# Moving the normalisation and turning of eight token tiles from the second layer's start into the first layer's attention

## The chip, the cores and the metric

The kernel is one program on one core of a Trainium2 chip. The metric is its time on the device in microseconds (us), the median of several runs. Its engines are TensorE (PE in the profile; PEld is its loading of weights), VectorE (DVE), ScalarE (ACT), GpSimd (POOL) and SyncE (SP, which here issues nearly all DMAs). Each engine executes its own instructions in order and waits on semaphores for the others.

## The reference

A two-layer backbone over 1024 latent tokens and 256 context tokens of width 1024, float32. The first layer's mixer is a windowed grouped-query attention, the second's a latent attention; each layer is `x += gate * mixer(norm(x) * (1 + scale) + shift)`.

```python
for i in range(DEPTH):                       # DEPTH = 2
    hx = rms_norm(x, norm_g[i]) * (1.0 + scale_x[:, None]) + shift_x[:, None]
    hc = rms_norm(ctx, norm_g[i]) * (1.0 + scale_c) + shift_c
    if kind == 0:
        yx, yc = window_gqa(hx, hc, a_w_in[j], a_sink[j], a_w_out[j], cos_a, sin_a, need_ctx)
    elif kind == 1:
        yx, yc = latent_attention(hx, hc, b_w_in[j], b_q_norm[j], ..., need_ctx)
    x = x + gate_x[:, None] * yx
    if need_ctx:
        ctx = ctx + gate_c * yc
return rms_norm(x, final_g)

def latent_attention(...):
    def project(h):
        cq, ckv, kr, g = jnp.split(h @ w_in, [...], axis=-1)
        q = (rms_norm(cq, q_norm) @ w_uq)...
        kv = (rms_norm(ckv, kv_norm) @ w_ukv)...
    ...
```

What matters here is the seam: the second layer needs h = norm(x1) * A + B of the first layer's output x1, transposed, so that the model width lies on partitions, for its input products `h @ w_in`.

## The kernel before

All on-chip memory is managed by hand: `arena_f` (float32) and `arena_r` (the operands of products) are cut into frames with `f_at(offset in KB, ...)` and `r_at`, and a `Ring` hands out a list of frames in turn. A ring of three frames therefore lets the fourth user start only when the first is done with its frame. `PB` is the accumulator memory (PSUM) of eight banks; `Banks` hands banks out in turn. Float32 products are made of three products of high and low parts (`mm3`, L126 to L128); `split` (L121, L122) makes such parts: a cast on ACT gives the high part, a subtract on DVE or POOL the low part.

The tokens are ten tiles of 128, two of context (0 and 1) and eight latent ones. The attention of the first layer runs over 40 units (`units`), a tile times one of four key groups, in the tile order `ORDER = (2, 0, 3, 1, 4, 5, 6, 7, 8, 9)`. A unit computes scores (L586), a masked maximum on DVE (L597), the exponential on ACT (L600), the transposes of P on PE (`T`, L617; split by L121 on ACT and L122 on DVE), the product with V (`PV`, L627) and its finish (`fin`, `fin2`). The output projection of a tile (`outproj`, L126 to L128 with 512 columns) is a generator, advanced a few products at a time between the steps of the next tile's units (`filler`). Its end multiplies by the gate (L674), adds to x (L675) and stores the tile of x1 (L676). The last tile's projection runs behind the last unit (`last_outproj`), and its second half accumulates in bank 0.

Behind it the second layer starts. `fetch1` loads weights in pieces through the ring `stg` (L264) and splits them; `build_x` handles a pair of tiles p: `norm_x` loads a tile of x1 (L212), sums its squares on ACT (L214), takes the reciprocal root (L215 on DVE, L216 on POOL) and scales the tile on DVE (L217); `turn_x` transposes it in eight steps on PE (L224) and copies two PSUM banks out on ACT (L225). `build_h` makes h of the pair: eight affine steps on DVE (L238), four casts on ACT (L241) and four subtracts (L243). Then `kv_tile` (24 products of 288 columns a tile, a norm at L958 to L997, transposes at L1010) runs over the ten tiles and `g_tile` (48 products of 256 columns) after each second latent one; between them, ahead of tile ti, tile ti + 3 is turned, and its pair's h is built. The written order is not the executed one to the letter: a scheduler merges the instructions of an engine, so places are shown below as they stand in the engines' own queues.

Of the kernel before, what the change touches and what calls it, by code (L numbers as in the profile page):

```python
# [60 lines left out]
def kernel(ctx: ExitStack, tc: tile.TileContext, t, out, dbg=None):  # L61
# [14 lines left out]
    x1_d = dpool.tile([TOK, D], F32, name="x1_d")  # L76
    qn_d = dpool.tile([8, 128, 2, SEQ], F32, name="qn_d")
# [132 lines left out]
    def norm_x(src, xr, junk):  # L210
        x = xr.next()
        load(out=x, in_=src)  # L212
        st = sm_ring()
# [4 lines left out]
        return x  # L218

    def turn_x(x, xt, j):  # L220
        for q in range(2):
            ps = shp(pst(), 4, 128)
            for c in range(4):
                nc.tensor.transpose(ps[:, c, :], x[:, (4 * q + c) * 128 : (4 * q + c + 1) * 128], ident)  # L224
            nc.scalar.copy(xt[:, 4 * q : 4 * q + 4, j * 128 : j * 128 + 128], ps)  # L225

    def build_x(p, src, xr, xtr, junk):

        xt = shp(xtr.next(), 8, 256)
        for j in range(2):  # L230
            turn_x(norm_x(src(2 * p + j), xr, junk), xt, j)
        return xt

    def build_h(p, xt, hT, A, B, fast=False, ks=range(8)):

        w = 1 if p == 0 else 0
        for k in ks:
            nc.vector.tensor_scalar(xt[:, k, :], xt[:, k, :], A[:, k, w : w + 1], B[:, k, w : w + 1], ALU.mult, ALU.add)  # L238
            if k % 2:
                hi = hT[:, 0, k - 1 : k + 1, :]  # L240
                nc.scalar.copy(hi, xt[:, k - 1 : k + 1, :])  # L241
                eng = nc.vector if fast or k % 4 == 1 else nc.gpsimd
                eng.tensor_sub(hT[:, 1, k - 1 : k + 1, :], xt[:, k - 1 : k + 1, :], hi.bitcast(F32))  # L243
# [434 lines left out]
    units = [UnitA(ti, g) for ti in ORDER for g in range(4)]  # L678

# [193 lines left out]
    for ui, u in enumerate(units):  # L873
# [11 lines left out]
        for ci in range(u.m):  # L885
# [90 lines left out]
    fetch1(1)  # L976
# [123 lines left out]
    nx = norm_x(src1(4), xr, junk)  # L1100
    for ti in range(NT):
        n = ti + 3
        if 4 <= n < NT:
            if n % 2 == 0:
                xt = shp(xtr.next(), 8, 256)
            turn_x(nx, xt, n % 2)
            if n + 1 < NT:
# [568 lines left out]
```

## Time and profile before

| | |
|---|---|
| median of 3 runs (lowest, highest) | 1596.19 us (1595.39, 1599.35) |
| profiled execution | 1596.15 us |
| its span | 1594.4 us |
| mean granted TensorE clock | 0.997 |
| PE, DVE, ACT, POOL busy, share of the span | 98%, 57%, 49%, 47% |
| last product with V of the attention (L627) starts | 715.68 us |
| output projection of the last tile (PE) | 716.28 to 730.47 us |
| first kv product of the second layer | 730.47 us |

Times in rows are microseconds from the start of the span. A wait row gives engine, buffer and line, the releasing engine and line, then the total in us, the number of times, and the longest. In a row of groups the mean duration in ns stands behind the busy time. A timeline row has start, duration, engine, line, operation, and in brackets idle time of the engine before it with what ended it.

### The profile page before, as it was taken

The page shows a single profiled execution, that of the slowest core. Times are in us where ns is not written, and L with a number is a line of the kernel's source. Part 1 is how long each engine was busy: PE and PEld are TensorE (multiplying, and loading weights), DVE is VectorE, ACT ScalarE, POOL GpSimd, SP SyncE. Part 2 cuts the span into 40 slices and gives each one's busy share as a digit, 9 for nine tenths or more (in the row PEclk, how much of TensorE's full clock was granted, in tenths as well). Part 3 has the DMA queues.
Part 4 walks back from the last instruction along what each step waited for, and adds up shares of the span by engine and source line. Part 5 has one row for each costly group of instructions (what it writes and reads, how often), then busy time and mean ns, then how long its engine had stood idle before and what let it go on. Part 6 is the DMA issues. An engine that isn't in the chain of part 4 may idle for free.

```text
span 1594.4 us, 26916 instructions
## 1 busy us (share of the span) xinstructions
PE 1555.2 (98%) x9938; PEld 1222.6 (77%) x9938; DVE 905.9 (57%) x1629; ACT 777.0 (49%) x1478; POOL 742.1 (47%) x805
## 2 busy tenths in 40 slices
PE   7899999999999999998999999999999999999998
PEld 4787777887878888887998899766766766766687
DVE  3515551618777777768525302667677677667454
ACT  3522232348777777767523332455545555555322
POOL 1231112115664444454113350388688688689510
PEclk9999999999999999999999999999999999999999
DMA  7446776354333333327113753313232233244251
GB/s 253 166 138 196 233 210 190 97 153 120 109 110 94 97 93 94 93 79 244 35 34 106 262 184 94 103 30 101 69 96 80 76 88 96 67 130 118 67 167 66
DMA packets 147203, 192.82 MB, mean 121 GB/s; under 512 B 13936, under 2 KB 84080, under 8 KB 147072
## 3 DMA queue, kind: packets, MB, share of 16 engines
q1 hardware_dynamic: 145456, 188.94, 39.5%
q10 hardware_dynamic: 1616, 2.17, 0.5%
q8 instruction: 78, 1.28, 0.4%
q14 instruction: 53, 0.43, 0.1%
HBM read 144.90 MB, written 46.15 MB: 120 GB/s over the span
## 4 chain that ended last, share of the span: by engine, by line
PE 86%; issue 2%; DVE 2%; POOL 2%; ACT 2%; DMA 1%; SPq 0%; POOLq 0%; DVEq 0%; ACTq 0%
PE PB L126 15%; PE PB L127 14%; PE PB L128 14%; PE PB L1303 11%; PE PB L1325 8%; PE PB L586 5%; PE PB L627 4%; PE PB L1266 4%; PE PB L617 4%; PE PB L183 1%; PE PB L1274 1%; PE PB L1354 1%; PE PB L646 1%; ACT arena_r L121 1%; DVE arena_r L122 1%
## 5 line engine op out<-in xcount | busy, mean ns | idle before, releaser
L126 PE MATMUL PB<-arena_r 128*128 128x512 f32 (+3 forms) x1496 | 509.9, 342 | 4.9 <-POOL arena_r L653 2.0
L127 PE MATMUL PB<-arena_r 128*128 128x512 f32 (+3 forms) x1496 | 502.4, 336 | 4.2 <-DVE arena_r L390 2.1
L128 PE MATMUL PB<-arena_r 128*128 128x512 f32 (+3 forms) x1496 | 500.3, 335 | 0.3 <-DVE arena_r L122 0.3
L1317 POOL TENSOR_TENSOR arena_f<-arena_f 128x512 f32<-128x512 f32 x252 | 328.3, 1303 | 82.1 <-ACT arena_f L1309 65.3
L126 PEld LDWEIGHTS PB<-arena_r 128*128 128x128 f32 x1496 | 283.7, 190 | 52.7 <-issue 12.5
L127 PEld LDWEIGHTS PB<-arena_r 128*128 128x128 f32 x1496 | 284.5, 190 | 32.0 <-DVE arena_r L390 3.5
L128 PEld LDWEIGHTS PB<-arena_r 128*128 128x128 f32 x1496 | 284.5, 190 | 28.3 <-DVE arena_r L122 0.5
L122 POOL TENSOR_TENSOR arena_r<-arena_f,arena_r 128x512 fp32r<-128x512 f32 x88 | 115.2, 1325 | 299.7 <-ACT arena_r L121 255.5
L1309 ACT ACTIVATE arena_f<-PB 128x1024 f32<-128x1024 f32 x160 | 164.1, 1027 | 108.9 <-PE PB L1303 65.9
L1268 DVE TENSOR_REDUCE arena_f<-PB 128x1 f32<-128x1024 f32 x128 | 156.1, 1219 | 86.7 <-PE PB L1266 86.6
L1303 PE MATMUL PB<-arena_r 64*128 64x512 f32 (+1 forms) x1600 | 202.3, 392 | 0.3 <-ACT arena_f L1309 0.3
L1303 PEld LDWEIGHTS PB<-arena_r 64*128 64x128 f32 (+1 forms) x1600 | 146.1, 185 | 31.5 <-ACT arena_f L1309 1.8
L122 DVE TENSOR_TENSOR arena_r<-PB,arena_r 128x512 fp32r<-128x512 f32 (+1 forms) x186 | 124.2, 674 | 61.9 <-ACT arena_r L121 61.0
L1325 PE MATMUL PB<-arena_f 128*64 128x512 f32 x640 | 144.4, 597 | 0.0
L600 ACT ACTIVATE arena_f<-arena_f,small 128x640 f32<-128x640 f32 (+2 forms) x160 | 119.5, 747 | 35.4 <-DVE small L597 32.7
L597 DVE CUSTOM_DVE_ANT_0 arena_f<-PB,arena_f,small 128x640 f32<-128x640 f32 (+2 forms) x176 | 125.2, 722 | 20.1 <-PE PB L586 12.6
L121 ACT CAST arena_r<-PB 128x512 fp32r<-128x512 f32 (+1 forms) x186 | 105.3, 573 | 47.4 <-PE PB L617 45.2
L121 ACT CAST arena_r<-arena_f 128x512 fp32r<-128x512 f32 (+3 forms) x141 | 83.8, 603 | 86.7 <-PE PB L128 12.5
L627 PE MATMUL PB<-arena_r 128*128 128x512 f32 x336 | 115.8, 429 | 0.5 <-DVE arena_f L639 0.5
L586 PE MATMUL PB<-arena_r 128*128 128x256 f32 (+1 forms) x576 | 111.0, 308 | 1.6 <-DVE small L597 1.3
L1325 PEld LDWEIGHTS PB<-arena_f 128*64 128x64 f32 x640 | 43.1, 136 | 83.2 <-issue 79.9
L617 PE MATMUL PB<-ident,arena_f 128*128 128x128 f32 x672 | 104.2, 274 | 1.3 <-DVE arena_r L122 0.8
(177 smaller groups left out, 1842.9 us busy)
## 6 DMA issues: line engine op xcount, KB each, us to landing
arena_f<-ada_w SPq DMA_DIRECT2D x47, 512.0 KB, 5.4
arena_r<-q_d SPq DMA_DIRECT2D x80, 256.0 KB, 3.9
arena_r<-qn_d SPq DMA_DIRECT2D x64, 256.0 KB, 3.9
arena_r<-qr_d SPq DMA_DIRECT2D x192, 64.0 KB, 3.3
arena_f<-a_w_in SPq DMA_DIRECT2D x40, 256.0 KB, 3.6
arena_f<-x SPq DMA_DIRECT2D x16, 512.0 KB, 6.6
g_d<-arena_f SPq DMA_DIRECT2D x32, 256.0 KB, 2.1
q_d<-arena_f SPq DMA_DIRECT2D x64, 128.0 KB, 2.4
```

Source lines behind the costliest of these rows:

```text
L121: nc.scalar.copy(hi, src)
L122: (lo_eng or nc.vector).tensor_sub(lo, src, hi.bitcast(F32))
L126: nc.tensor.matmul(o, ah, bh, start=first, stop=False)
L127: nc.tensor.matmul(o, al, bh, start=False, stop=False)
L128: nc.tensor.matmul(o, ah, bl, start=False, stop=last)
L586: nc.tensor.matmul(S[:, at : at + n], qT[:, s, hq, :], kT[:, g, k : k + n], start=s == 0, stop=s == 1)
L617: nc.tensor.transpose(pt[:, h, :], self.Ps[h][:, ci * 128 : ci * 128 + 128], ident)
L627: nc.tensor.matmul(self.pv, V[:, self.chunks[ci], self.g, :], PT[:, s], start=ci == 0 and s == 0, stop=ci == self.m - 1 and s == 1,)
L1303: nc.tensor.matmul(S[:, t], k[r, c : c + 128], q[r], start=j == 0, stop=j == 4)
L1309: nc.scalar.activation(E, self.S, AF.Exp)
L1317: eng.tensor_add(self.acc, self.acc, E[:, t])
L1325: nc.tensor.matmul(self.pv[p : p + 64], Vq[:, cs[t], self.h % 4, :], E[:, t], start=i == 0, stop=i == 4)
```

## The change

Tiles 0 to 7 are normalised and turned inside the attention, by a generator `pre_turns` that is advanced behind the tiles at positions 5 to 9 of `ORDER` (two steps a unit, one at position 8). Its steps per tile are: load x1 into `xpre` and, a step later, the scaling; then four transposes, a PSUM copy into one of two staging buffers `tpre` and a store to DRAM (`xT_d`), twice. The turned pairs are loaded back in two halves of 512 KB each (`load_xt`): pair 0 at unit 38, pairs 1 and 2 at the start of the second layer, pair 3 ahead of the kv tiles. Only tiles 8 and 9 are turned between the kv tiles, as before. `build_h` works on halves of a pair (four affine steps, two casts, two subtracts); pairs 2, 3 and 4 are built in halves behind kv tiles 0, 1, 2, 3, 5 and 6 (`part`). The weights of block 1 (for cq) are fetched behind tile 3, not ahead of the loop. To make room, the weight ring `stg` (three frames still), the gate ring `gr` and other frames move.

```diff
@@ helpers
     def norm_x(src, xr, junk):
         x = xr.next()
         load(out=x, in_=src)
+        scale_x(x, junk)
+        return x
+
+    def scale_x(x, junk):
         st = sm_ring()
         ...
-            nc.scalar.copy(xt[:, 4 * q : 4 * q + 4, j * 128 : j * 128 + 128], ps)
+            nc.scalar.copy(xt[q][:, :, j * 128 : j * 128 + 128], ps)
-    def build_x(p, src, xr, xtr, junk):
-        ...
     def build_h(p, xt, hT, A, B, fast=False, ks=range(8)):
         ...
-            nc.vector.tensor_scalar(xt[:, k, :], xt[:, k, :], A[:, k, w : w + 1], ...)
+            x = xt[k // 4][:, k % 4, :]
+            nc.vector.tensor_scalar(x, x, A[:, k, w : w + 1], B[:, k, w : w + 1], ALU.mult, ALU.add)
@@ attention
-    or1, rtr = (Ring(F, [o, o - 5], 256) for o in (43, 45))
+    or1, rtr = Ring(F, [43, 44], 256), Ring(F, [45, 41], 256)
-    gr = Ring(F, [2.5, 34, 46], 256)
+    gr = Ring(F, [34, 35, 46], 256)
+    xpre, tpre = f_at(48, 1024), [f_at(o, 4, 128) for o in (36, 38)]
+
+    def pre_turn(ti):
+        load(out=xpre, in_=x1_d[ti * 128 : ti * 128 + 128, :])
+        yield
+        scale_x(xpre, f_at(36, 512).bitcast(BF16))
+        yield
+        for q in range(2):
+            ps = shp(pst3(), 4, 128)
+            for c in range(4):
+                k = 4 * q + c
+                nc.tensor.transpose(ps[:, c, :], xpre[:, k * 128 : k * 128 + 128], ident)
+            nc.scalar.copy(tpre[q], ps)
+            ts = slice(ti % 2 * 128, ti % 2 * 128 + 128)
+            load(out=xT_d[ti // 2, :, 4 * q : 4 * q + 4, ts], in_=tpre[q])
+            yield
+    ...
+    xt_at = [[f_at(o, 4, 256) for o in os] for os in ((48, 36), (14, 18), (22, 26), (14, 18), (22, 26))]
+
+    def load_xt(p):
+        for q in range(2):
+            load(out=xt_at[p][q], in_=xT_d[p, :, 4 * q : 4 * q + 4, :])
@@ end of each unit
+        for _ in range({5: 2, 6: 2, 7: 2, 8: 1, 9: 2}.get(ui // 4, 0)):
+            next(pre, None)
+        if ui == 38:
+            load_xt(0)
         u.fin(og)
@@ second layer
-    junk = f_at(34.5, 512).bitcast(BF16)
-    stg = Ring(F, [30, 32.25, 49.5], 576)
-    xr = Ring(F, [22, 26, 45], 1024)
-    xtr = Ring(F, [14, 37], 2048)
+    junk = f_at(40, 512).bitcast(BF16)
+    stg = Ring(F, [30, 32, 44], 512)
+    xr = Ring(F, [48, 36], 1024)
     fetch1(0, nc.vector)
-    xts = {0: build_x(0, src1, xr, xtr, junk)}
-    build_h(0, xts.pop(0), hT1[0], ada1.A, ada1.B, fast=True)
-    xts[1] = build_x(1, src1, xr, xtr, junk)
-    build_h(1, xts.pop(1), hT1[1], ada1.A, ada1.B, fast=True)
+    load_xt(1)
+    build_h(0, xt_at[0], hT1[0], ada1.A, ada1.B, fast=True)
+    load_xt(2)
+    build_h(1, xt_at[1], hT1[1], ada1.A, ada1.B, fast=True)
     ...
     fetch1(6)
-    fetch1(1)
-    nx = norm_x(src1(4), xr, junk)
+    load_xt(3)
+    nx = {8: norm_x(src1(8), xr, junk)}
     for ti in range(NT):
-        n = ti + 3
-        if 4 <= n < NT:
-            ...
+        if ti in (4, 5):
+            turn_x(nx[ti + 4], xt_at[4], ti % 2)
         kv_tile(ti)
         flush(2)
+        part = {0: (2, 0), 1: (2, 4), 2: (3, 0), 3: (3, 4), 5: (4, 0), 6: (4, 4)}
+        if ti in part:
+            p, k = part[ti]
+            build_h(p, xt_at[p], hT1[p], ada1.A, ada1.B, True, range(k, k + 4))
+        if ti == 1:
+            nx[9] = norm_x(src1(9), xr, junk)
+        if ti == 3:
+            fetch1(1)
         if ti > 1 and ti % 2:
             g_tile(6, ti // 2)
-    qst = Ring(F, [16, 20, 24, 37, 41, 45], 1024)
+    qst = Ring(F, [16, 20, 24, 36, 48, 8], 1024)
```

Most line numbers shift: the three products are L127 to L129 in the changed kernel, the subtract of a split L123, the affine step L236, the subtract of h L242, the gate multiply L673, the x1 store L675, the weight loads L263; the pre-turning transposes are L689, their stores L692, the load of x1 for them L681, the reload L703.

The first place is PE's queue where the output projection of the last tile ends and the kv products of the second layer start (512 columns are the projection, 288 the kv tiles, L224 the turning). Before:

```order
L126 MATMUL PB<-arena_r 128x288
L127 MATMUL PB<-arena_r 128x288
L128 MATMUL PB<-arena_r 128x288
L126 MATMUL PB<-arena_r 128x288
L224 MATMUL PB<-ident,arena_f 128x128 x8
L127 MATMUL PB<-arena_r 128x288
```

Now:

```order
L128 MATMUL PB<-arena_r 128x512
L129 MATMUL PB<-arena_r 128x512
L127 MATMUL PB<-arena_r 128x288
L128 MATMUL PB<-arena_r 128x288
L129 MATMUL PB<-arena_r 128x288
```

The turning transposes, which stood between and among the kv products, are gone from here, so one kind of product follows the other directly.

They stand in the attention instead; this is PE in one of the last units (L616 transposes of P, L626 the product with V, L585 scores, L645 the finish):

```order
L626 MATMUL PB<-arena_r 128x512 x2
L585 MATMUL PB<-arena_r 128x256 x4
L689 MATMUL PB<-ident,arena_f 128x128 x4
L585 MATMUL PB<-arena_r 128x256 x4
L616 MATMUL PB<-ident,arena_f 128x128 x3
L645 MATMUL PB<-ident,arena_f 128x128 x2
L616 MATMUL PB<-ident,arena_f 128x128
L585 MATMUL PB<-arena_r 128x256 x2
L616 MATMUL PB<-ident,arena_f 128x128
```

The four L689 are half a tile's turning, between score products.

The second place is DVE's queue around the gate multiply of the last output projection (L674, then the add L675; L673 and L674 now). Subtracts of 288 columns belong to kv weights, L238 (L236 now) and L243 (L242 now) to h, L217 and L215 to the norm of a tile. Before:

```order
L243 TENSOR_TENSOR arena_r<-arena_f,arena_r 128x512
L238 TENSOR_SCALAR arena_f<-arena_f,small 128x256 x2
L217 TENSOR_SCALAR arena_f<-arena_f,small 128x1024
L215 TENSOR_SCALAR small<-small 128x1
L674 TENSOR_TENSOR arena_f<-PB,arena_f 128x512
L243 TENSOR_TENSOR arena_r<-arena_f,arena_r 128x512
L217 TENSOR_SCALAR arena_f<-arena_f,small 128x1024
L675 TENSOR_TENSOR arena_f<-arena_f 128x512
L215 TENSOR_SCALAR small<-small 128x1
L674 TENSOR_TENSOR arena_f<-PB,arena_f 128x512
L217 TENSOR_SCALAR arena_f<-arena_f,small 128x1024
```

Now:

```order
L242 TENSOR_TENSOR arena_r<-arena_f,arena_r 128x512
L236 TENSOR_SCALAR arena_f<-arena_f,small 128x256
L242 TENSOR_TENSOR arena_r<-arena_f,arena_r 128x512
L123 TENSOR_TENSOR arena_r<-arena_f,arena_r 128x288 x2
L673 TENSOR_TENSOR arena_f<-PB,arena_f 128x512
L236 TENSOR_SCALAR arena_f<-arena_f,small 128x256
L674 TENSOR_TENSOR arena_f<-arena_f 128x512
L236 TENSOR_SCALAR arena_f<-arena_f,small 128x256
L673 TENSOR_TENSOR arena_f<-PB,arena_f 128x512
L123 TENSOR_TENSOR arena_r<-arena_f,arena_r 128x288
L674 TENSOR_TENSOR arena_f<-arena_f 128x512
L1003 TENSOR_SCALAR arena_f<-arena_f 128x512
```

The norm's steps left; two subtracts of weights and h of the second pair now stand directly ahead of the first multiply, and affine steps stand between the two multiplies.

The third place is SP's queue around the first weights of the second layer (x_d<- is a store of a tile of x1, <-x_d the load of a tile of x1, xT_d the turned tiles, b_w_in weights, g_d and q_d the attention's operands, <-x the projection's residual). Before:

```order
L676 DMA x_d<-arena_f 128x1024
L658 DMA arena_f<-x 128x1024
L570 DMA arena_f<-g_d 128x2x128 x2
L212 DMA arena_f<-x_d 128x1024
L264 DMA arena_f<-b_w_in 128x288 x2
L212 DMA arena_f<-x_d 128x1024
L676 DMA x_d<-arena_f 128x1024
L264 DMA arena_f<-b_w_in 128x288 x3
L212 DMA arena_f<-x_d 128x1024
L658 DMA arena_f<-x 128x1024
L264 DMA arena_f<-b_w_in 128x288 x2
L212 DMA arena_f<-x_d 128x1024
```

Now:

```order
L703 DMA arena_f<-xT_d 128x1024
L692 DMA xT_d<-arena_f 128x4x128 x2
L703 DMA arena_f<-xT_d 128x1024 x4
L263 DMA arena_f<-b_w_in 128x288 x2
L703 DMA arena_f<-xT_d 128x1024
L675 DMA x_d<-arena_f 128x1024
L263 DMA arena_f<-b_w_in 128x288 x3
L657 DMA arena_f<-x 128x1024
L263 DMA arena_f<-b_w_in 128x288 x2
L703 DMA arena_f<-xT_d 128x1024
L263 DMA arena_f<-b_w_in 128x288
L703 DMA arena_f<-xT_d 128x1024
```

The loads of x1 between the weights have become reloads of turned halves; five of those of the first pairs, and the last two stores of turned halves, stand ahead of the first weights.

More of the change, by code (lines that the diff above doesn't have):

```diff
@@ L76 @@
     x1_d = dpool.tile([TOK, D], F32, name="x1_d")
+    xT_d = dpool.tile([4, 128, 8, 256], F32, name="xT_d")
     qn_d = dpool.tile([8, 128, 2, SEQ], F32, name="qn_d")
@@ L678, with pre_turns @@
     units = [UnitA(ti, g) for ti in ORDER for g in range(4)]
+    xpre, tpre = f_at(48, 1024), [f_at(o, 4, 128) for o in (36, 38)]
[13 more added lines that the diff above has]
+            yield
+    def pre_turns():
+        for ti in range(8):
+            yield from pre_turn(ti)
+    xt_at = [[f_at(o, 4, 256) for o in os] for os in ((48, 36), (14, 18), (22, 26), (14, 18), (22, 26))]
+    def load_xt(p):
+        for q in range(2):
+            load(out=xt_at[p][q], in_=xT_d[p, :, 4 * q : 4 * q + 4, :])
+    pre = pre_turns()
     def wo_load():
```

18 lines of the change are left out of this document (3 added, 15 removed).

## The prediction

> **What bounds the kernel now.** I read the head of the page first, then its chain, then busy time by stretches around the hand-over from the first layer to the second, and last what TensorE (PE) waited for there.
>
> ```profile
> span 1594.4 us, 26916 instructions
> PE 1555.2 (98%) x9938; PEld 1222.6 (77%) x9938; DVE 905.9 (57%) x1629; ACT 777.0 (49%) x1478; POOL 742.1 (47%) x805
> PE 86%; issue 2%; DVE 2%; POOL 2%; ACT 2%; DMA 1%; SPq 0%; POOLq 0%; DVEq 0%; ACTq 0%
> ```
>
> The profiled execution took 1596.15 us, 1.75 us more than its span and practically the median of the three runs (1596.19), so a difference worked out in the trace can be put on the median as it stands. PE is busy 98% of the span and carries 86% of the chain: only PE work removed, or PE idle time closed or opened, moves the end. Columns below: stretch, its length, busy time of PE, PEld, DVE, ACT and POOL, the granted TensorE clock, DMA share, GB/s.
>
> ```profile
> 520.00:640.00 120.00, 119.80 (x717) 103.06 (x716) 92.19 (x185) 87.56 (x203) 58.85 (x102) 1.00 0.33 93
> 716.00:731.00 15.00, 14.40 (x72) 11.26 (x71) 12.26 (x32) 12.28 (x27) 3.01 (x4) 1.00 0.89 295
> 731.00:804.00 73.00, 65.83 (x510) 64.43 (x509) 49.77 (x127) 41.01 (x89) 25.12 (x35) 0.98 0.35 107
> 804.00:900.00 96.00, 95.69 (x636) 87.09 (x635) 35.30 (x69) 26.01 (x54) 24.76 (x24) 1.00 0.37 113
> ```
>
> The first attention (here 520 to 640) leaves PE 0.2 us idle in 120; behind 804 it is full again. Between lie 88 us with about 7.8 us of idle PE and a clock under 1. That is the stretch in which all ten tiles are normalised and turned now. The waits in it, each once:
>
> ```profile
> PE PB L1010 <- ACT arena_f L225: 3.3, 1, 3.3
> PE PB L224 <- DVE small L959: 1.2, 1, 1.2
> PE PB L126 <- ACT arena_r L241: 1.1, 1, 1.1
> PE PB L224 <- DVE arena_f L217: 0.9, 1, 0.9
> PE PB L127 <- DVE arena_r L243: 0.6, 1, 0.6
> PE PB L224 <- DVE small L215: 0.5, 1, 0.5
> ```
>
> All six belong to the chain norm, transposes, affine, cast, subtract of a tile (L215 to L243), or stand behind it. The longest also costs clock:
>
> ```profile
> 755.00:758.20 3.20, 0.00 (x0) 0.00 (x0) 3.20 (x9) 2.62 (x6) 0.00 (x0) 0.92 0.58 157
> 758.20:760.00 1.80, 1.77 (x9) 1.78 (x10) 1.80 (x7) 1.77 (x6) 0.10 (x1) 0.50 0.00 0
> 760.00:762.00 2.00, 2.00 (x14) 2.00 (x14) 1.66 (x6) 1.07 (x3) 1.53 (x3) 0.72 0.00 0
> ```
>
> **What goes.** The six waits are 3.3 + 1.2 + 1.1 + 0.9 + 0.6 + 0.5 = 7.6 us. The half clock loses 1.80 x 0.50 + 2.00 x 0.28 = 1.46, say 1.4. Together 9.0 us, if nothing takes their place.
>
> **What moves.** 64 of the 80 PE transposes go into the attention, where PE is full, so they cost there what they save later.
>
> ```profile
> 716.28 0.91 PE L126 MATMUL PB<-arena_r 128*128 128x512 f32 x2
> 725.69 0.39 PE L126 MATMUL PB<-arena_r 128*128 128x512 f32 x1
> 730.47 0.29 PE L126 MATMUL PB<-arena_r 128*128 128x288 f32 x1
> 730.60 0.29 PE L127 MATMUL PB<-arena_r 128*128 128x288 f32 x1
> 731.61 1.09 PE L224 MATMUL PB<-ident,arena_f 128*128 128x128 f32 x8
> 732.45 0.38 PE L127 MATMUL PB<-arena_r 128*128 128x288 f32 x1
> ```
>
> Eight take 732.45 - 731.61 = 0.84 us, so 64 are 6.7 us on either side: zero in the sum. A 128x288 product is issued every 0.13 us (730.60 - 730.47), a 128x512 one every 0.228 (21 of them from 725.69 to 730.47).
>
> **What the attention pays.** Per tile it also gets a Square, two PSUM copies, a scaling on DVE and a reciprocal root on POOL; 1.06 + 0.19 + 2 x 0.59 = 2.4 us of ACT and 0.75 of DVE, by these groups (mean ns in the middle):
>
> ```profile
> L225 ACT COPY arena_f<-PB 128x512 f32<-128x512 f32 x20 | 11.2, 585 | 2.4 <-PE PB L224 2.4
> L214 ACT ACTIVATE arena_f<-arena_f 128x1024 bf16<-128x1024 f32 x10 | 10.6, 1059 | 0.7 <-DMA arena_f<-x_d 0.5
> L214 ACT ACTIVATION_READ_ACCUMULATOR arena_f<-arena_f 128x1 f32 x10 | 1.9, 190 | 0.0
> L217 DVE TENSOR_SCALAR arena_f<-arena_f,small 128x1024 f32<-128x1024 f32 x10 | 7.5, 753 | 4.5 <-POOL small L216 4.4
> ```
>
> ACT is 73% busy there (87.56 of 120) and would be 77 to 79%. What counts is how far it runs ahead of PE:
>
> ```profile
> ACT arena_r L121 <- PE PB L617: 27.8, 47, 0.8
> DVE arena_r L122 <- ACT arena_r L121: 34.0, 46, 1.7
> PE PB L617 <- ACT arena_f L600: 0.2, 1, 0.2
> ```
>
> These are of 520 to 700. Before its cast of a transposed P tile, ACT stands 27.8 / 47 = 0.59 us waiting for PE, so a Square of 1.25 us can make a cast 0.66 late, and a copy of 0.59 can just be swallowed. Eight Squares give at most 5.3 us. Against that, output-projection products stand between the transposes of P and their use, and the 0.2 us row shows no lateness with the attention's own copies in place. I take 0.15 us a tile, 1.2 us, nearest to that row; ends 0 and 5.3. The pre-transposes share two PSUM banks with the transposes of P (a part of the same term: a bank is held by a 0.59 copy as it is by the 0.59 cast). DMA: 8 loads of 512 KB move forward; 16 stores of 256 KB and 8 loads of 512 KB are new, on the one SP queue, past the q and gate loads. The share there is 0.33; nothing of PE waits for a load in these rows, so 0. POOL, busy 58.85 us of 120, gets one 128x1 operation a tile: 0.
>
> **At the end of the attention.** DVE does affine steps in 0.35 us each (725.23), in 0.70 where POOL works on tiles beside it (751.16):
>
> ```profile
> 715.95 0.69 DVE L674 TENSOR_TENSOR arena_f<-PB,arena_f 128x512 f32<-128x512 f32 x1 [1.07 <-PE PB L128]
> 725.23 1.38 DVE L238 TENSOR_SCALAR arena_f<-arena_f,small 128x256 f32<-128x256 f32 x4 [0.54 <-ACT arena_f L225]
> 751.16 5.60 DVE L238 TENSOR_SCALAR arena_f<-arena_f,small 128x256 f32<-128x256 f32 x8
> ```
>
> Four of them, for tile pair 1, stand now ahead of the last subtract of P: 1.4 us, less part of the 1.07 that DVE idles there. I take 0.5; ends 0 and 2.8 (four at 0.70).
>
> **The new first wait.** (Times on the clock of the trace before, the moved 6.7 us left out.) Without transposes the output projection of tile 9 takes 48 x 0.228 = 10.9 us from 716.3, so PE is at the kv products at 727.2 instead of 730.47, and 13 of them later (1.7 us) at 728.9. Then it needs PSUM bank 0, which the multiply of the output projection empties on DVE (L674; L673 in the changed kernel). That one now stands behind the subtracts of the last two kv weight pieces:
>
> ```profile
> 723.84 0.80 SPq L264 DMA_DIRECT2D arena_f<-b_w_in  x2
> 727.59 0.43 ACT L121 CAST arena_r<-arena_f 128x288 fp32r<-128x288 f32 x1 [0.20 <-DMA arena_f<-b_w_in]
> 728.58 0.69 DVE L243 TENSOR_TENSOR arena_r<-arena_f,arena_r 128x512 fp32r<-128x512 f32 x1
> 729.18 0.45 DVE L122 TENSOR_TENSOR arena_r<-arena_f,arena_r 128x288 fp32r<-128x288 f32 x1
> 731.64 0.69 DVE L674 TENSOR_TENSOR arena_f<-PB,arena_f 128x512 f32<-128x512 f32 x1
> 744.42 0.42 DVE L973 TENSOR_SCALAR arena_f<-arena_f 128x512 f32<-128x512 f32 x1
> ```
>
> The weights are issued at 723.84, cast from 727.59 (3.75 us later), subtracted until 729.6. A ring of three buffers holds them back, and it has three in the new kernel too, so these times stay; without the 0.6 us between the two subtracts, they end at 729.1. Behind come a multiply, two affine steps, an add, and the second multiply; at the 0.6 us at which such operations follow each other (728.58 to 729.18) 0.6 + 2 x 0.35 + 0.6 + 0.6 = 2.5, which makes 731.6 or 731.7. PE stands from 728.9 to 731.7: 2.8 us. Ends: 0 (before, PE lost nothing to weights, its transposes lying over that time) and 4.3, if the landing takes 1.5 us longer because the reloads of the turned tiles share the DMA engines (their share is 0.89 in this stretch).
>
> **The new second wait.** In place of the 3.3 us, the first transpose of a normalised kv tile waits for its DVE chain, behind the scaling of b_q_norm (L973), a load that lands late, and behind h of pair 2. ACT issues that load at 732.81 now and some 3.2 us earlier, 729.6, without the last Squares and copies ahead of it (two tiles at 2.4 us, less ACT's waits); the nearest row for its landing is the last:
>
> ```profile
> 732.81 0.38 ACTq L972 DMA_DIRECT2D arena_f<-b_q_norm  x1
> arena_f<-b_kv_norm ACTq DMA_DIRECT2D x1, 128.0 KB, 5.3
> ```
>
> 729.6 + 5.3 = 734.9; with 0.42 for the scaling, three subtracts (2.0), five affine steps at 0.35 to 0.70 (2.6) and the tile's own norm (1.4, an estimate from the 1.2 us that PE waits on such a norm now) it is about 741.3. PE has 72 - 13 = 59 products left from 731.7, to 739.6. Idle 1.8 us; ends 0 and 3.5.
>
> The sum: -9.0 + 1.2 + 0.5 + 2.8 + 1.8 = -2.7, so 1596.2 - 2.7 = 1593.5 us. The loop behind, with h in halves (four affine steps and two subtracts on DVE between two kv tiles, not eight and four), I cost at nothing: a half is 4 x 0.35 to 0.70 + 2 x 0.69 = 2.8 to 4.2 us of DVE, and the cover is a kv tile of 24 x 0.13 = 3.2 us and, behind each odd one, a gate tile. If that cover failed, the 1.0 us over, four times, would be added. The second layer's weights for cq, fetched later (behind tile 3), are first read behind the whole loop: 0.
>
> **The clock, weighed.** Row: 3.3 us of idleness gave 0.50; the other waits, up to 1.2 us, cost no clock, since the 1.46 us lost behind it are all of the 0.02 that 731 to 804 lacks. The new 2.8 us lies between; with the clock kept the sum is 1593.5, with it lost 1594.9. [...]
>
> **Rivals.**
> (1) The cover holds: weights and b_q_norm come early enough, and the two new waits are 0.5 us each. -9.0 + 1.2 + 0.5 + 1.0 = -6.3: 1590. For it: in the stretch ACT has 24 operations fewer, DVE 16. Against: the 3.75 us from issue to cast has a row. Chance 0.30.
> (2) The new waits are as long as the old. With bank 0 at +4.3 (over 3.3, so the clock falls: 1.4) and 3.0 at the second: -9.0 + 1.2 + 0.5 + 4.3 + 1.4 + 3.0 = +1.4: 1597.6. For it: DMA share 0.89. Chance 0.20.
> (3) Slower: the Squares land on casts that PE needs. It decides when a cast becomes late by over 1.0 us a tile: 8 x 1.25 (no slack at all) = 10 in place of 1.2, so -2.7 + 8.8 = +6.1: 1602.3. For it: ACT executes in order, at 73%. Against: 0.59 us of slack per cast, and PE's 0.2. Chance 0.12.
> The likeliest stays the sum, 1593.5 (chance 0.38, between 1590.8 and 1596).
>
> **From chances to numbers.** A measurement tells 0.3%, 4.8 us, from no change, so faster means below 1591.4 and slower above 1601.0. Faster: rival 1, and the low end of the sum, 0.30 + 0.08 = 0.38. Slower: rival 3 and the high end of rival 2, 0.12 + 0.03 = 0.15. Same: the rest, 0.47. The range goes from 1587.5 (every new term near its lower end: -9.0 makes 1587.2) to 1601.0 (rival 2 with three tenths of what rival 3 adds to the attention, 1597.6 + 2.6 = 1600.2, and up to the bound of slower); it leaves out the 0.15 above and 0.05 below.
>
> **What would show it.** In the trace after: PE's waits at L1010 on the copy L225 and the 0.50 clock are gone (first step); the attention 6.7 us longer, with PE waits under 2 us (second); kv products from about 727 + 6.7, with one wait near the 13th (third) and one at the first transpose of a kv tile (fourth). Wrong if PE waits on casts (L122) in the attention row by row, or if no wait stands where the weights arrive.

## The result: 1.3% slower, and the profile after

The changed kernel takes 1617.26 us (1615.89 to 1620.10), the kernel before, with one run more than the prediction had, 1597.73 us; the ratio is 1.0126, 95% interval 1.0105 to 1.0147. The forecast was 1593.5, with a range up to 1601.0. The head of the page after:

```profile
span 1616.0 us, 26933 instructions
PE 1562.3 (97%) x9938; PEld 1225.6 (76%) x9938; DVE 890.8 (55%) x1629; ACT 776.5 (48%) x1478; POOL 747.2 (46%) x805
PE 77%; issue 5%; DVE 4%; POOL 4%; ACT 3%; DMA 3%; POOLq 0%; SPq 0%; DVEq 0%; ACTq 0%
```

PE's share of the chain fell from 86% to 77%: other engines and transfers hold PE up now. To see where, I cut each span at two marks that all kernels have, the issue of the x1 store of tile 1 and that of tile 8. Between them lies the attention with the turning (called S below), behind them the rest. Before, then after, in the columns of the prediction's stretches:

```profile
524.13:718.04 193.91, 193.27 (x1154) 165.28 (x1153) 146.30 (x297) 139.31 (x327) 97.75 (x166) 1.00 0.31 91
718.04:1594.40 876.36, 858.34 (x5921) 654.64 (x5919) 493.46 (x740) 391.65 (x609) 475.05 (x405) 1.00 0.35 105
```

```profile
524.42:748.10 223.68, 206.15 (x1221) 172.81 (x1220) 159.35 (x329) 159.23 (x366) 104.03 (x174) 0.99 0.43 126
748.10:1616.00 867.90, 850.75 (x5854) 648.63 (x5852) 465.50 (x709) 370.99 (x569) 473.69 (x397) 0.99 0.35 103
```

The rest gained 8.5 us (876.36 - 867.90). S lost 29.8: PE is busy 12.9 us longer and idle 17.5 us instead of 0.6. What PE waited for in S after:

```profile
PE PB L585 <- DVE small L596: 7.2, 3, 2.9
PE PB L616 <- DVE arena_r L123: 4.7, 4, 1.7
PE PB L626 <- DVE arena_f L638: 4.4, 4, 2.9
```

These three rows are 16.3 of the 17.5 us, all on VectorE, at scores, transposes of P and products with V. The 2.9 us in the last row are one wait at the end of the attention, which is taken up below. What VectorE and ScalarE themselves waited for in the turning (L219 Square, L220 mean, L221 root on POOL, L222 scaling):

```profile
DVE small L220 <- ACT arena_f L219: 18.4, 7, 3.7
ACT arena_f L219 <- DMA arena_f<-x_d: 6.4, 4, 2.5
ACT arena_f L219 <- DMA xT_d<-arena_f: 5.7, 3, 2.1
DVE arena_f L222 <- POOL small L221: 4.9, 8, 0.7
```

VectorE stood 18.4 + 4.9 = 23.3 us. In its queue mean and scaling follow each other directly in seven of the eight tiles, with the attention's work behind them:

```order
L123 TENSOR_TENSOR arena_r<-PB,arena_r 128x512
L220 TENSOR_SCALAR small<-small 128x1
L222 TENSOR_SCALAR arena_f<-arena_f,small 128x1024
L123 TENSOR_TENSOR arena_r<-PB,arena_r 128x512
L596 ISA arena_f,small<-PB,arena_f,small 128x640
```

One such place in the timelines of SP, ACT, DVE and PE:

```profile
572.81 0.41 SPq L681 DMA_DIRECT2D arena_f<-x_d  x1
578.26 1.06 ACT L219 ACTIVATE arena_f<-arena_f 128x1024 bf16<-128x1024 f32 x1 [1.59 <-DMA arena_f<-x_d]
579.44 0.15 DVE L220 TENSOR_SCALAR small<-small 128x1 f32<-128x1 f32 x1 [2.05 <-ACT arena_f L219]
580.27 0.75 DVE L222 TENSOR_SCALAR arena_f<-arena_f,small 128x1024 f32<-128x1024 f32 x1 [0.68 <-POOL small L221]
582.48 1.03 PE L585 MATMUL PB<-arena_r 128*128 128x256 f32 x4 [2.06 <-DVE small L596]
```

The load of the tile is issued at 572.81, after the tile before has left its frame, and the Square starts on it 5.45 us later. ScalarE has reached the Square and waits; VectorE waits for the Square from 577.4 on, then for the root; the subtract and the maximum that PE needs run only behind the scaling, and PE stands 2.06 us.

### The profile page after: what moved, and what is told of

Read it like the earlier page. It is cut to its first block, busy times and chain, and to the rows that moved or that the text cites. A ratio compares the mean times of both kernels' runs of the same rounds, so it can differ in the third digit from the quotient of the medians.

```text
span 1616.0 us, 26933 instructions
## 1 busy us (share of the span) xinstructions
PE 1562.3 (97%) x9938; PEld 1225.6 (76%) x9938; DVE 890.8 (55%) x1629; ACT 776.5 (48%) x1478; POOL 747.2 (46%) x805
## 4 chain that ended last, share of the span: by engine, by line
PE 77%; issue 5%; DVE 4%; POOL 4%; ACT 3%; DMA 3%; POOLq 0%; SPq 0%; DVEq 0%; ACTq 0%
PE PB L127 14%; PE PB L128 13%; PE PB L129 13%; PE PB L1334 11%; PE PB L1356 8%; PE PB L1297 4%; PE PB L585 3%; PE PB L626 3%; PE PB L616 2%; DVE arena_r L123 1%; DMA xT_d<-arena_f 1%; PE PB L184 1%; DVE arena_f L596 1%; ACT arena_r L122 1%; PE PB L1305 1%
## 5 line engine op out<-in xcount | busy, mean ns | idle before, releaser
L127 PE MATMUL PB<-arena_r 128*128 128x512 f32 (+3 forms) x1496 | 510.0, 342 | 5.0 <-POOL arena_r L652 2.0
L129 PE MATMUL PB<-arena_r 128*128 128x512 f32 (+3 forms) x1496 | 501.0, 335 | 0.2 <-DVE arena_r L123 0.2
L1348 POOL TENSOR_TENSOR arena_f<-arena_f 128x512 f32<-128x512 f32 x252 | 324.6, 1288 | 79.4 <-ACT arena_f L1340 62.6
L127 PEld LDWEIGHTS PB<-arena_r 128*128 128x128 f32 x1496 | 284.5, 191 | 52.6 <-issue 12.5
L129 PEld LDWEIGHTS PB<-arena_r 128*128 128x128 f32 x1496 | 285.4, 191 | 28.3 <-DVE arena_r L123 0.5
L123 POOL TENSOR_TENSOR arena_r<-arena_f,arena_r 128x512 fp32r<-128x512 f32 x88 | 115.4, 1325 | 309.6 <-ACT arena_r L122 255.5
L123 DVE TENSOR_TENSOR arena_r<-PB,arena_r 128x512 fp32r<-128x512 f32 (+1 forms) x186 | 123.6, 673 | 53.0 <-ACT arena_r L122 52.0
L626 PE MATMUL PB<-arena_r 128*128 128x512 f32 x336 | 118.8, 435 | 5.6 <-DVE arena_f L638 4.8
L585 PE MATMUL PB<-arena_r 128*128 128x256 f32 (+1 forms) x576 | 113.3, 311 | 8.7 <-DVE small L596 8.4
L122 ACT CAST arena_r<-PB 128x512 fp32r<-128x512 f32 (+1 forms) x186 | 105.1, 572 | 30.8 <-PE PB L616 29.8
L616 PE MATMUL PB<-ident,arena_f 128*128 128x128 f32 x672 | 106.4, 275 | 5.8 <-DVE arena_r L123 5.5
```

What stands on the lines that cost most here:

```text
L122: nc.scalar.copy(hi, src)
L123: (lo_eng or nc.vector).tensor_sub(lo, src, hi.bitcast(F32))
L127: nc.tensor.matmul(o, ah, bh, start=first, stop=False)
L129: nc.tensor.matmul(o, ah, bl, start=False, stop=last)
L585: nc.tensor.matmul(S[:, at : at + n], qT[:, s, hq, :], kT[:, g, k : k + n], start=s == 0, stop=s == 1)
L626: nc.tensor.matmul(self.pv, V[:, self.chunks[ci], self.g, :], PT[:, s], start=ci == 0 and s == 0, stop=ci == self.m - 1 and s == 1,)
```

## The experiments

Lengths of S, PE's idle time in S (length less busy, from the same view), the part of S in which the trace's record of the granted clock has 0.50, and the rest, in us, each from one profiled execution; the time is the median of the runs. The part ahead of S, which no edit is about, differs between these executions by up to 4.3 us (522.6 to 527.0), so the columns don't add up to differences of the medians.

| kernel | time | S | idle in S | half clock in S | rest |
| --- | --- | --- | --- | --- | --- |
| before | 1597.7 | 193.9 | 0.6 | 0 | 876.4 |
| after | 1617.3 | 223.7 | 17.5 | 3.4 | 867.9 |
| e1 no norm | 1600.2 | 204.3 | 2.2 | 0 | 867.9 |
| e2 norm on GpSimd | 1609.8 | 217.8 | 10.4 | 10.2 | 868.0 |
| e3 no transposes | 1596.3 | 204.5 | 8.4 | 0 | 866.7 |
| e4 own frame for the Square | 1616.4 | 221.9 | 15.1 | 6.8 | 867.7 |
| e5 spread | 1602.3 | 207.5 | 3.8 | 0 | 868.1 |
| e6 early load | 1604.0 | 210.9 | 7.3 | 0 | 867.2 |
| e7 (the order of e5) | 1603.9 | 207.6 | 3.7 | 0 | 866.7 |
| e8 late b_q_norm | 1618.0 | 227.1 | 16.8 | 13.7 | 864.2 |
| e9 chain cut | 1614.0 | 216.4 | 8.4 | 10.2 | 867.6 |
| e10 places held | 1601.3 | 206.6 | 3.5 | 0 | 868.8 |
| e11 spread, late b_q_norm | 1602.7 | 207.5 | 4.0 | 0 | 869.2 |
| e12 places held, late b_q_norm | 1599.6 | 207.1 | 4.3 | 0 | 865.6 |
| e13 no wait for transfers | 1600.1 | 205.4 | 2.8 | 3.4 | 868.0 |
| e14 no wait for transfers, chain cut | 1599.8 | 205.8 | 3.3 | 3.4 | 869.9 |
| e15 halves alone, on before | 1597.1 | 193.9 | 0.6 | 0 | 876.2 |
| e16 halves, late b_q_norm, on before | 1598.3 | 193.9 | 0.6 | 0 | 876.6 |

In all of them a scheduler orders the queues anew, so an edit can also move instructions that it does not name; where that matters, it is said.

**e1: the norm left out.**

```diff
-        scale_x(xpre, f_at(36, 512).bitcast(BF16))
```

> The changed kernel with the norm of the eight tiles (sum of squares on ScalarE, two steps and the scaling on VectorE, reciprocal root on GpSimd) left out of the attention; loads, transposes, copies, stores and reloads stay, so the second layer's input of these tiles is not normalised. Theory A (VectorE stands in its queue until the Square on ScalarE is done, and the attention's maxima and subtracts stand behind it; 23 us of such waits in the trace after): the attention gets back most of its 22 us of stalls, time about 1597. Rival B (the turning itself: 64 transposes and 16 copies share two PSUM banks with the transposes of P): the loss stays, 1612 or more. Rival C (the 32 added DMAs delay loads): the loss stays, 1612 or more.

Measured 1600.16 us, ratio to before 1.0011 (1.0000 to 1.0022). The idle time in S falls from 17.5 to 2.2 us. Transposes, copies and all 32 transfers are still there, so B and C fall as sole causes. The forecast of theory A, about 1597, was 3 us too low.

**e2: the norm's VectorE steps on GpSimd.**

```diff
-        nc.vector.tensor_scalar(st[:, 1:2], st[:, 0:1], 1.0 / D, EPS, ALU.mult, ALU.add)
+        eng.tensor_scalar(st[:, 1:2], st[:, 0:1], 1.0 / D, EPS, ALU.mult, ALU.add)
...
-        nc.vector.tensor_scalar_mul(x, x, st[:, 2:3])
+        eng.tensor_scalar_mul(x, x, st[:, 2:3])
...
-        scale_x(xpre, f_at(36, 512).bitcast(BF16))
+        scale_x(xpre, f_at(36, 512).bitcast(BF16), nc.gpsimd)
```

The default of `eng` stays VectorE, so the edit moves the steps of the eight tiles in the attention alone; the two tiles turned later, which the expectation also names, keep theirs on VectorE.

> The changed kernel with the norm's two VectorE steps (mean plus epsilon, and the scaling of 128x1024) on GpSimd instead, in the attention and in the two tiles turned later. Theory A: VectorE no longer stands for the Square, and most of the 22 us come back, 1597 to 1603 (ScalarE still stands for the load of the tile, some 12 us in all, part of which PE feels). Rivals B and C: no change, 1612 to 1620.

Measured 1609.82 us (1.0076; 1.0047 to 1.0105), above the forecast of theory A but 7 us under the changed kernel. VectorE stands for the Square no longer; GpSimd (21.9 us) and ScalarE do, and PE waits 9.3 us for the attention's finish (L638).

**e3: the transposes left out.**

```diff
-                nc.tensor.transpose(ps[:, c, :], xpre[:, k * 128 : k * 128 + 128], ident)
-            nc.scalar.copy(tpre[q], ps)
+            nc.scalar.copy(tpre[q], shp(xpre[:, q * 512 : q * 512 + 512], 4, 128))
```

> The changed kernel with the 64 transposes left out of the attention: ScalarE copies the normalised tile itself, not its transpose from PSUM, into the staging buffer; norm, stores and reloads stay, so the second layer computes with tiles that are not turned. Theory A: PE work falls by 64 x 0.105 = 6.7 us and the stalls stay, 1609 to 1612. Rival B: the stalls go as well, about 1590 to 1595. Rival C: 1609 to 1612 as in A.

Measured 1596.27 us (0.9988; 0.9976 to 0.9999): a miss for theory A as I had put it. The idle time halved, to 8.4 us. But VectorE's wait for the Square also fell, from 18.4 to 4.8 us, since the order had moved with the edit. So this run did not hold the norm's waits fixed, and cannot speak for B.

**e4: the Square's unused output in its own frame.**

```diff
-    gr = Ring(F, [34, 35, 46], 256)
+    gr = Ring(F, [2.5, 40, 46], 256)
-        scale_x(xpre, f_at(36, 512).bitcast(BF16))
+        scale_x(xpre, f_at(34, 512).bitcast(BF16))
```

> The changed kernel with the unused output of the Square in a frame of its own instead of the first staging buffer (the gate ring moves to make room), so the Square no longer waits for the store of the tile before. In the trace after, ScalarE waits 5.7 us for these stores (3 times) and 6.4 us for the loads of x1 (4 times). Theory A: up to 5.7 us come back, 1611 to 1615. If the waits for the load take over, or if the stall is B or C: 1616 to 1618.

Measured 1616.39 us (1.0117; 1.0088 to 1.0146). The waits for stores are gone and those for loads took their place: 12.2 us in 7 waits, against 6.4 in 4. That is what the second branch of the expectation had.

**e5, e6, e7: the steps spread over two units.**

```diff
-        for _ in range({5: 2, 6: 2, 7: 2, 8: 1, 9: 2}.get(ui // 4, 0)):
-            next(pre, None)
+            for _ in range(plan.get(slot, 0) if pre else 0):   # behind each chunk
+                next(pre, None)
+            slot += 1
...
+    plan = {0: 1, 4: 1, 5: 1, 6: 1, 8: 1, 9: 1}    # e5
+    plan = {0: 1, 4: 3, 8: 1, 9: 1}                # e6
+    plan = {4: 4, 8: 1, 9: 1}                      # e7
```

> The changed kernel with the turning of the eight tiles emitted in six steps spread over the chunks of two units: load at the first chunk, Square at the fifth, mean and root at the sixth, scaling at the seventh, the two halves of the transposes at the ninth and tenth; the Square's unused output has its own frame. Nothing is left out. Theory A' (the steps of one tile stand next to each other in in-order queues, so ScalarE stands for the load, VectorE for the Square and the root, PE for the rest): the attention's stalls fall from 22 us to a few, time 1594 to 1600. Rival D (what costs is the sum of the added work on the two PSUM banks and ScalarE, wherever it stands): 1610 or more.

> As the spread version, but Square, mean, root and scaling are emitted together at the fifth chunk; only the load of the tile is ahead by four chunks. A': VectorE still stands for the Square and the root, some 2 us a tile, of which PE feels part, so 1598 to 1608, between the spread version and the one without the early load. If only the late load cost time: equal to the spread version. D: 1610 or more.

> Control for the two others: as the spread version, but load, Square, mean, root and scaling are emitted together at the fifth chunk, the transposes as there. A': ScalarE stands for the landing of the load and VectorE behind it, 1608 to 1620. If the mere place of the transposes in the unit decided, it would equal the spread version.

All three also have the frames of e4, which alone gained no more than 0.9 us (1616.39 against 1617.26). Measured 1602.32 (1.0027; 1.0018 to 1.0037), 1604.02 (1.0039; 1.0023 to 1.0055) and 1603.91 us (1.0043; 1.0032 to 1.0054). The control e7 failed: the scheduler put its instructions into exactly the order of e5 in every queue, so the two are one kernel timed twice, and their ratios are 0.16% apart: a difference of that size between two versions means nothing yet. What e5 shows holds all the same: VectorE's wait for the Square is 3.8 us instead of 18.4, the idle time in S 3.8 instead of 17.5, with nothing left out. e6 lies where A' had it, but its time is not told from e7; what tells it from e5 is the trace, with 7.5 us of VectorE's wait for the Square and 7.3 us of idle PE. Its loads are not out of the way either: ScalarE still waits 6.1 us for them.

**e8: the scaling of b_q_norm behind the kv loop.**

```diff
     load2(out=qn, in_=t["b_q_norm"].partition_broadcast(128))
-    nc.vector.tensor_scalar_mul(qn, qn, B_SCALE)
...
+    nc.vector.tensor_scalar_mul(qn, qn, B_SCALE)
     fetch1(2, nc.vector)
```

> The changed kernel with the scaling of b_q_norm emitted behind the loop over the kv tiles instead of ahead of it, so VectorE does not stand for that load there. My account of the second wait (the first transpose of a kv tile waits 4.5 us for VectorE, behind this scaling): the wait falls to 1 to 2 us and the half clock behind it goes, 2.5 to 5 us less than the changed kernel, 1612 to 1615. If the wait comes from h and the weights on VectorE alone: 1616 to 1618.

Measured 1617.97 us (1.0127; 1.0107 to 1.0148). In its place it did what was expected (the wait fell from 4.5 to 2.4 us, the rest from 867.9 to 864.2), but S came out 3.5 us longer, with less idle PE: 13.7 us of it ran at half clock instead of 3.4. By my estimate (half of the 10.3 us) that is about 5 us more; PE's busy time in S is 4.2 us longer (210.38 against 206.15). e11 adds it to e5, e12 to e10, e16 to the halves below.

**e9: the chain cut.**

```diff
-        scale_x(xpre, f_at(36, 512).bitcast(BF16))
+        nc.scalar.activation(f_at(36, 512).bitcast(BF16), gx, AF.Square, accum_out=st[:, 0:1])
+        nc.vector.tensor_scalar(st[:, 1:2], mhalf, 1.0 / D, EPS, ALU.mult, ALU.add)
+        nc.gpsimd.tensor_tensor(st[:, 2:3], st[:, 1:2], mhalf, ALU.pow)
+        nc.vector.tensor_scalar_mul(xpre, xpre, mhalf)
```

> The changed kernel with every operation of the turning in place, but the chain of the norm cut: the Square reads the gate frame (always there) instead of the loaded tile, and the two VectorE steps read constants, so VectorE waits neither for the Square nor for the root; loads, transposes, copies, stores and reloads as they are. The second layer computes with tiles that are scaled wrongly. Theory A (standing in the queues): the stalls go though no operation does, 1596 to 1603. Rival D (the amount of added work on ScalarE, PSUM banks and DMA): 1612 to 1618 as before.

Measured 1614.04 us (1.0110; 1.0091 to 1.0128), which reads like D. Its waits of VectorE and ScalarE tell why not:

```profile
DVE arena_f L687 <- DMA arena_f<-x_d: 9.8, 6, 2.8
ACT arena_f L684 <- DMA xT_d<-arena_f: 5.7, 3, 2.0
```

With the chain cut, the scaling waits for the load itself. The idle time in S fell by half, 17.5 to 8.4; 5 us of the rest go in e14 below, where the scaling waits for no load. The half clock grew from 3.4 to 10.2 us, which by the same estimate gives back about 3.4 us of what the idle time gained; PE's busy time grew by 1.9 us (208.00 against 206.15).

**e10, e11, e12: places held.** The Square is queued behind the newest exponential, mean and scaling behind the newest maximum:

```diff
+        with tc.issue_after(lastA[0].ins):
+            nc.scalar.activation(f_at(34, 512).bitcast(BF16), xpre, AF.Square, accum_out=st[:, 0:1])
...
+        with tc.issue_after(lastV[0].ins):
+            nc.vector.tensor_scalar_mul(xpre, xpre, st[:, 2:3])
```

> The spread version with its places made to hold: the Square is queued behind the exponential that is newest when it is emitted, the mean and the scaling each behind the newest maximum of the scores on VectorE, so that three or four VectorE instructions of the attention stand between mean and scaling (in the spread version they stand next to each other, and VectorE waits 0.68 us for the root between them in each tile). Nothing is left out. A: VectorE's 3.8 + 5.4 us of standing go, and PE's idle time in the attention falls from 3.8 us to 1 or 2: 1598 to 1601. D: as the spread version, 1602 to 1604.

> The spread version with the scaling of b_q_norm emitted behind the kv loop. In the changed kernel this took the wait at the first transpose of a kv tile from 4.5 to 2.4 us and the second layer's part of the time down by 3.7 us. If the two add: 1598 to 1600. If the spread version's wait there (5.1 us) has another cause: 1602.

> Both: places made to hold in the attention, and the scaling of b_q_norm behind the kv loop. If both gains add, 1594 to 1598, equal to the kernel before, since the 64 transposes cost 6.7 us in the attention and save 6.7 us later, and the waits that went and came are about as long; below 1592 only if the removed waits of the second layer's start are worth more than the trace shows.

Measured 1601.27 (1.0029; 1.0017 to 1.0041), 1602.73 (1.0036; 1.0022 to 1.0049) and 1599.55 us (1.0016; 1.0007 to 1.0024). e10 took VectorE's standing for mean and scaling from 9.2 to 1.8 us, but the idle time of PE only from 3.8 to 3.5; the forecast of 1 to 2 missed. e11 gained nothing on e5. e12, forecast at 1594 to 1598, is the best that does all the work with the eight tiles in the attention; it is 0.16% above the kernel before, no more than e5 and e7 differ by.

**e13, e14: no waits, all the work.**

```diff
-        load(out=xpre, in_=x1_d[ti * 128 : ti * 128 + 128, :])
+        load(out=cp_d[ti * 128 : ti * 128 + 128, :], in_=x1_d[ti * 128 : ti * 128 + 128, :])
```

In e14 mean and scaling read constants besides, as in e9.

> The changed kernel with the loads of x1 going to a scratch place in DRAM instead of the tile's frame (same bytes read, same queue), and the Square's unused output in its own frame: Square, mean, root and scaling stand in their chain as before, but work on what lies in the frame and wait for no transfer. The second layer's input of eight tiles is wrong. Theory A1 (the queues stand because the load, or the store of the tile before, comes late): most stalls go, 1599 to 1604. A2 (the chain ScalarE, VectorE, GpSimd, VectorE itself, 2 us a tile, is what VectorE stands for): 1608 to 1616. D (amount of work): 1612 to 1618.

> As e13, and with the chain cut as in e9: VectorE's two steps read constants. Every operation and every byte is still there, and neither ScalarE nor VectorE has anything of the turning to wait for. A1 and A2: 1597 to 1602 (the 64 transposes, 16 copies and the rest of the added work alone). D: 1612 to 1618.

Measured 1600.12 (1.0014; 1.0005 to 1.0024) and 1599.80 us (1.0014; 1.0004 to 1.0023). The stretch S of e13, and the one wait for the Square that is left in it:

```profile
525.19:730.62 205.43, 202.62 (x1217) 172.78 (x1215) 158.41 (x327) 157.95 (x363) 105.62 (x173) 0.99 0.43 130
DVE small L221 <- ACT arena_f L220: 0.6, 3, 0.2
```

ScalarE is as busy as in the changed kernel (157.95 against 159.23 us) and VectorE too (158.41 against 159.35), the DMA share is the same 0.43, and the idle time is 2.8 us instead of 17.5. D and C are out as the cause of the lost idle time: standing, and not work, made it. Of the idle time that is left, 2.7 us (e13) and 3.0 us (e14) are the one wait at the end of the attention. e13 does not tell the late transfers from the chain, since with no load to wait for, the first load is issued some 98 us earlier and the scaling stands 24 to 74 rows behind the mean. The changed kernel, e9 (chain cut) and e14 (transfers gone too) have 17.5, 8.4 and 3.3 us of idle PE, 9 us for the chain and 5 for the transfers in that order of taking them away. Since the Square at the head of the chain itself waits for the load, and each edit moved other instructions too, the runs give no split that is free of that order.

**e15, e16: h in halves alone, on the kernel before.**

```diff
-                build_h(n // 2, xt, hT1[n // 2], ada1.A, ada1.B, fast=True)
+                build_h(n // 2, xt, hT1[n // 2], ada1.A, ada1.B, fast=True, ks=range(4))
         kv_tile(ti)
         flush(2)
+        if 4 <= n < NT and n % 2:
+            build_h(n // 2, xt, hT1[n // 2], ada1.A, ada1.B, fast=True, ks=range(4, 8))
```

> The kernel before with one part of the change alone: h of the pairs 2 to 4 is built in two halves, the first ahead of the kv tile and the second behind it; all tiles are turned where they were. If the 3.3 us wait at the first transpose of a kv tile (and the half clock behind it, 1.4 us) came from VectorE being held by eight affine steps and four subtracts in a row: 2 to 5 us less than before, 1592 to 1595. If the wait only moves to the second half: no change.

> The kernel before with h in halves and the scaling of b_q_norm behind the kv loop. If that scaling holds VectorE here too: another 0.5 to 2 us less than the version with halves alone, 1591 to 1594. If it doesn't matter where transposes still fill the start: as the version with halves alone.

Measured 1597.07 and 1598.32 us, each 1.0002 (0.9993 to 1.0011): no change. The wait at L1010 stays in e15, without the half clock (1.00 from 716 to 804, where the kernel before has 0.98), and in place of 0.5 us PE now waits 1.8 us for another tile's norm:

```profile
PE PB L1010 <- ACT arena_f L225: 3.1, 1, 3.1
PE PB L224 <- DVE small L215: 1.8, 2, 1.2
716.00:804.00 88.00, 79.19 (x576) 74.30 (x575) 61.35 (x157) 52.60 (x115) 30.10 (x39) 1.00 0.44 143
```

No version that does all the work beat the kernel before; e3, 0.12% under it, leaves the transposes out.

## Why the prediction was wrong

**The step that failed is "What the attention pays", 1.2 us with an upper end of 5.3.** The trace shows 29.8 less the moved 6.7, 23.1 us, of which 2.9 belong to the next term, the end of the attention; some 20 are left. I had priced the added operations by their own duration against the slack of a cast, and costed the loads at nothing because "nothing of PE waits for a load in these rows". Both take for granted that the operations are ready when their turn comes. They form a chain through load, ScalarE, VectorE, GpSimd and VectorE again, and its members stood side by side in queues that the attention shares. The transfer alone takes 5.3 to 6.1 us here; L220 and L222 stand side by side in VectorE's queue whatever the times, and I did not follow what they wait for. e5 (nothing left out; other places and the Square's own frame) and e13 and e14 (all the work, no waits for the norm's input) show that this is it. The missing question was the one for any added wait: what is queued behind it.

Where the 29.8 went, by the view: 16.9 us more idle time, and 12.9 of PE work. The transposes have this row, and two of their groups these places:

```profile
L689 PE MATMUL PB<-ident,arena_f 128*128 128x128 f32 x64 | 9.7, 278 | 0.0
568.05 0.66 PE L689 MATMUL PB<-ident,arena_f 128*128 128x128 f32 x4
568.47 0.48 PE L585 MATMUL PB<-arena_r 128*128 128x256 f32 x2
568.79 0.60 PE L689 MATMUL PB<-ident,arena_f 128*128 128x128 f32 x4
569.14 0.60 PE L585 MATMUL PB<-arena_r 128*128 128x384 f32 x2
```

The busy time of 9.7 counts stretches in which neighbours run as well (such rows of PE add up to 303 us in S, where PE is busy 206). By the start of the next product the two groups take 0.42 and 0.35 us, and all 64 transposes 6.8: the 6.7 of the prediction came true. Of the other 6.1 us, 1.7 are, by my estimate of half the stretch, the 3.4 us at half clock, and some 0.7 are three products of the output projection that S has more than before (250 against 247, at 0.228). The remaining 3.7 stay open. In e13 and e14, with the same half clock, S is 11.5 and 11.9 us longer than before, of which 2.2 and 2.6 are idle time and 9.3 work, so there less than 1 us stays open.

**The six waits and the half clock of the old start** went, 9.0 us; only at the first transpose of a kv tile does PE still wait for a turning copy (L229, 1.2 us). What came instead, with three places in VectorE's queue:

```profile
PE PB L1039 <- DVE arena_f L1026: 4.5, 1, 4.5
PE PB L626 <- DVE arena_f L638: 2.9, 1, 2.9
PE PB L1039 <- ACT arena_f L229: 1.2, 1, 1.2
PE PB L127 <- DVE arena_f L673: 1.1, 1, 1.1
734.55 1.46 DVE L236 TENSOR_SCALAR arena_f<-arena_f,small 128x256 f32<-128x256 f32 x4 [1.54 <-DMA arena_f<-xT_d]
737.97 1.95 DVE L236 TENSOR_SCALAR arena_f<-arena_f,small 128x256 f32<-128x256 f32 x4 [1.36 <-DMA arena_f<-xT_d]
764.42 0.43 DVE L1003 TENSOR_SCALAR arena_f<-arena_f 128x512 f32<-128x512 f32 x1 [3.61 <-DMA arena_f<-b_q_norm]
```

The first new wait (bank 0) was 1.1 us against 2.8; the second (L1039) 4.5 against 1.8, with another 1.2 and a half clock of 6.8 us that I had not expected; the end of the attention 2.9 against 0.5. There, ahead of the last steps, h of a pair not only takes its affine steps: VectorE also stands 1.54 and 1.36 us for the reload of the turned halves, the same mistake as above. The rest gained 8.5 us where the sum gave 9.0 + 6.7 - 2.8 - 1.8 = 11.1: near, by errors that partly cancel. By the view 7.6 of the 8.5 are PE work (858.34 - 850.75); PE's idle time in the rest fell by 0.9 us alone, since the new waits are nearly as long as the old. That b_q_norm holds the second wait is borne out in part: VectorE stands 3.61 us for its load, and without that e8 has 2.4 us of the wait left; but in e11 the same edit took it from 5.1 to 3.7, a wait of 1.8 for the copy came in its place, and the rest gained nothing on e5 (869.2 against 868.1).

**The clock.** The sum took it as kept behind a wait of 2.8 us. No run shows that term: the rows before have waits up to 1.2 us and one of 3.3, and this wait came out at 1.1. What the changed kernel shows is 2.06 us followed by half clock and 2.9 us not (last section); the wait at L1039, put at 1.8 us with no loss of clock, was 4.5 and had 6.8 us at half clock behind it.

**The halves costed at nothing**: borne out by e15 on the kernel before; in the changed kernel they were not tried alone.

**The rivals.** The third named the right place and sign, but its mechanism (a Square of 1.25 us makes a cast late) gave 10 us at most; what happened is that VectorE stood up to 3.7 us a time for it. It had a chance of 0.12. The first two were about the second layer's start, where little was decided.

## What to carry to other kernels

An operation moved into a stage that an in-order engine fills can cost, beyond its duration, the time from its turn in the queue to the end of what it depends on (here VectorE stood 23.3 us, and PE 17.5); follow the chain through every queue it crosses, transfers included, before pricing it. Space the links so that each is done when the next comes up: here places, with the Square's own frame (0.9 us alone), were worth 15 us. And where the moved work is PE work and both places are full of PE, the most that can be gained is the waits at the old place less the waits at the new.

## What the hardware showed that I had not expected

The clock did not follow the length of the idle time. In the changed kernel 2.06 us without a product (from 580.42) were followed by 3.4 us at half clock; 2.9 us at another place (from 738.5) were not; 4.5 us (from 767.9) were, by 6.8 us. PE's busy time stands behind the length, the granted clock before the last two numbers:

```profile
580.40:582.40 2.00, 0.01 (x1) 0.00 (x0) 2.00 (x5) 0.25 (x1) 0.00 (x0) 1.00 0.00 0
582.99:586.41 3.42, 3.42 (x13) 2.75 (x13) 2.50 (x6) 2.08 (x7) 0.00 (x0) 0.50 0.44 114
738.50:741.40 2.90, 0.00 (x0) 0.01 (x1) 2.85 (x8) 1.24 (x2) 0.30 (x1) 1.00 0.39 152
741.40:743.00 1.60, 1.57 (x9) 1.38 (x10) 1.60 (x4) 0.15 (x1) 1.43 (x3) 1.00 0.02 5
743.00:745.00 2.00, 2.00 (x11) 1.56 (x9) 2.00 (x4) 2.00 (x5) 0.45 (x1) 1.00 0.68 182
768.00:772.40 4.40, 0.01 (x1) 0.00 (x0) 3.49 (x10) 4.00 (x11) 2.08 (x3) 0.81 0.50 174
770.73:774.14 3.41, 1.65 (x7) 1.65 (x8) 2.52 (x8) 2.11 (x5) 3.16 (x4) 0.50 0.00 0
774.14:777.55 3.41, 3.41 (x17) 3.41 (x16) 3.41 (x7) 1.20 (x3) 2.11 (x2) 0.50 0.60 162
```

While the record has 0.50, PE starts a product of 288 columns every 0.24 us, and soon after it every 0.13:

```profile
776.34 0.44 PE L127 MATMUL PB<-arena_r 128*128 128x288 f32 x1
776.58 0.44 PE L128 MATMUL PB<-arena_r 128*128 128x288 f32 x1
777.82 0.29 PE L127 MATMUL PB<-arena_r 128*128 128x288 f32 x1
777.95 0.29 PE L128 MATMUL PB<-arena_r 128*128 128x288 f32 x1
```

So I estimate the loss at half of such a stretch: 1.7 us behind the 2.06 us of waiting, none behind the 2.9. What decides between the two is not shown; in these three places the length alone does not.
